# Attention's late work at other places of its steps, one table on a queue of its own, half of the first weight unit by VectorE, and the sums of k in one burst

## The chip, the cores and the metric

The kernel runs on one core of a Trainium2 chip. The metric is the device time of one execution in microseconds, from its first to its last instruction and a little around them. The core's engines are TensorE (PE, with its weight loads listed apart as PEld), VectorE (DVE), ScalarE (ACT), GpSimd (POOL) and SyncE (SP), which issues most of the transfers. Each works through its own list of instructions in order.

## What is computed

A trunk of two layers on 512 positions of width 1024, in float32. Layer 0 mixes by a Conformer convolution module, layer 1 by native sparse attention; a SwiGLU FFN of width 2816 follows each.

```python
for i in range(DEPTH):
    h = rmsnorm(x, norm_mix[i])
    y = conformer_conv_module(h, ...) if i % 4 == 0 else nsa_attention(h, ...)
    x = x + y
    x = x + swiglu_ffn(rmsnorm(x, norm_ffn[i]), ffn_w_in[i], ffn_w_out[i])
```

The attention has 16 heads of 64 in 4 groups and three branches, weighed by sigmoid gates: a compressed one (31 blocks of 32 positions, put through a small MLP), a selected one and a window. With 512 positions there are 8 blocks to select and up to 16 may be chosen, so selected and window are both plain causal attention, each with its own k and v.

```python
o_c = softmax(q @ k_cmp * scale, cmp_end <= t) @ v_cmp
o_s = softmax(q @ k_slc * scale, tok <= t) @ v_slc
o_w = softmax(q @ k_win * scale, 0 <= rel < 512) @ v_win
return g[0] * o_c + g[1] * o_s + g[2] * o_w
```

## The kernel before

The state x lies transposed, as eight tiles of 128 features by 512 positions. All weight products are made of split numbers: a factor is a high part (what the fast format of PE holds) and a low part, the rest, and one product is three matmuls (high by high, high by low, low by high). The weights come in units of up to 128x1024 through SP's queue as `wr`; ACT makes the high part `wh`, DVE the low part `wl` (`w_dma`, `w_hi`, `w_lo`, `next_w`, L244 to L281). Nearly all instructions run through one wrapper, so that their line in the profile is L153, and they are told apart by their tiles.

The start: `vec` (gains and biases) and x0 are the first two transfers of SP's queue, unit 0 is the third; ACT loads its function table in the meantime. For each of the eight x tiles ACT and DVE make `hh` and `hl`, and PE multiplies with units 0 to 3.

Layer 1's projections of q, k and v follow the FFN of layer 0. The tables `BESIDE` and `V_BESIDE` put side work beside the products of a unit: names such as `s0123` (sums of squares of k's tiles 0 to 3, tile `psq`) or `y0` and `e0` (parts of the compressed MLP), with the place in the unit.

Attention's main part is a loop over n = 1 to 17 (L2054 to L2090). There are 16 units of work, one for each pair (j, br): j is one of eight tiles of two heads, br the branch (1 selected, 2 window). Step n, three stages deep:

- scores of unit n: for each head (par 0, 1) and for t = 3, 2, 1, 0 the two matmuls of `S`, 128 query rows by 128(t+1) keys. DVE masks S into `Pm` and takes its peak `mx` in one custom instruction, ACT takes the exponential and its sum. Where br is 1, thus in even steps, t = 0 makes the columns for both branches, and the window's go to `P0` (a step with odd n has no score for t = 0). The S tiles go round three PSUM buffers.
- `weigh_late`: DVE's reciprocal of the sums, and on POOL two products that weigh Pm by it and by the gate.
- `flip` of unit n−1 (its heads are `ua`, `ub`): PE transposes blocks of Pm into `T`; `t2` and `t0` are copied out by ACT, `t1` by DVE. T shares three PSUM buffers (pool `p2`) with `psc`, `pct` and `bc`.
- `values` of unit n−2: twelve matmuls into `O`; after the second branch `out_parts` splits O into `oh` (ACT) and `ol` (DVE). `ol` and some other low parts are put off by `behind`, and issued at the next `catch_up`.

The order of each step is that of the code: S(0,3), S(0,2), S(0,1), a weigh, catch_up and values, S(0,0), flip t2, a fill, flip t1 of ua, a weigh, S(1,3), flip t1 of ub, a weigh, S(1,2), S(1,1), S(1,0), a weigh, a fill, flip t0 of ua and of ub, out_parts. Here S(p,t) is the score of head p. A fill is a piece of the list `FILL`, two to a step: the parts of the next pair of query tiles' compressed attention (`P1` to `P3`: scores `psc`, softmax by way of `cm`, `sc` and `cl`, transposes `pct`), norms `n4` to `n7` of q (`bc` among them, which DVE multiplies into `qraw`), k's later work, and at the end two weight units of the product to come (`w0`, `w1`). Within these steps every engine is held to the order of the program.

Of the kernel before, what the change touches and what calls it, by code (L numbers as in the profile page):

```python
# [19 lines left out]
P = 128  # L20
T = 512
# [71 lines left out]
    (("ga", "w", "s0", "s1 b1"), ("", "s2 s3 w", "gb s4 l", "s5 st1"), ("s6 l", "s7 l", "sc", "")))  # L93
# [4 lines left out]
FILL = ("tr0 P1.0  P1.1 P1.2  P1.3 P1.4  n4 P1.5+d3  k3+P2.0 n5  P2.1+d5 P2.2  k5 P2.4  n6 P2.5  P2.3 n7  "  # L98
        "P3.0 P3.1  P3.2 P3.3  wd P3.4  P3.5 w0  w1").split()
# [66 lines left out]
def trunk(ctx: ExitStack, tc: tile.TileContext, A, out):  # L166
# [77 lines left out]
    def w_dma(i):  # L244
        if i in raws or i >= len(units):
            return
        ap, cols, _ = units[i]
        t = wp.tile([P, 1024], F32, tag="wr", name=f"wr{i}")
        nc.sync.dma_start(t[:, :cols], ap)
        raws[i] = t  # L250
# [36 lines left out]
    nc.scalar.activation(dummy[:, :1], zb[:, :1], AF.Copy)  # L287
    vec = cst.tile([P, NVEC], F32, name="vec")
    nc.sync.dma_start(vec, A["vec"])
# [148 lines left out]
    def conv_module():  # L438
        acc = new_acc()
        with ExitStack() as cx:  # L440
# [33 lines left out]
            hold[0] = True  # L474
            for k in range(NK):
                if k < NK - 1:
                    split_x(k, V_NM0)
                if k == NK - 2:
                    split_x(NK - 1, V_NM0)
                if k % 2 == 0:  # L480
                    wh, wl = next_w(False)
                if k == 0:
                    load_tables()
                for m in range(2):
                    c = slice(k % 2 * 256 + m * P, k % 2 * 256 + (m + 1) * P)
                    mm3(pend[m], wh[:, c], wl[:, c], hh[k], hl[k], k == 0, k == NK - 1)
# [850 lines left out]
    def nsa(acc, cosT, sinT, gnext):  # L1337
# [140 lines left out]
        def square(e, ps):  # L1478
            sqs[e] = kp.tile([P, T], F32, tag="qsq", name=nm("qsq"), bufs=SQB)
            nc.scalar.activation(sqs[e], ps, AF.Square)  # L1480
# [76 lines left out]
        def split_1(q, eng):  # L1557

            hi, lo = (qk.tile([P, T], F32R, tag="q2", name=nm(z), bufs=Q2B) for z in ("qh", "ql"))
            if eng is nc.scalar:  # L1560
                eng.activation(hi, q, AF.Copy)
            else:
                eng.tensor_copy(hi, q)
            nc.gpsimd.tensor_tensor(lo, q, hi, ALU.subtract)
            return hi, lo

        def k_move(c):
            box["k2", c] = split_1(ks[c], nc.scalar)
# [82 lines left out]
        def q_pair(p):  # L1651
# [56 lines left out]
            if p == 0:  # L1708
                return move, scores, stacks, soft_a, soft_c, trans
            return [lambda: (move(0), scores(0)), lambda: (stacks(0), scores(1)), lambda: (move(1), soft_a()),  # L1710
                    lambda: stacks(1), soft_c, trans]
# [41 lines left out]
        extra["s0123"] = lambda: sums("k", range(4), 6)  # L1753
        extra["s45"] = lambda: sums("k", (4, 5), 6)
# [248 lines left out]
        fill_ = list(FILL)  # L2003
# [5 lines left out]
        def pair_(p, i):  # L2009
            if i == 0:  # L2010
                pairs[p] = q_pair(p)
            pairs[p][i]()

        for p in range(1, 4):
            for i in range(6):
                extra[f"P{p}.{i}"] = lambda p=p, i=i: pair_(p, i)
# [7 lines left out]
        def run_fill():  # L2024
            catch_up()
            if fill_:
                run(fill_.pop(0).replace("+", " "))
# [26 lines left out]
        for n in range(1, N + 2):  # L2054
# [9 lines left out]

            sc_(0, 3, 2, 1)
            weigh_late()
            if n > 1:
                catch_up()
                values(U.pop(n - 2))
            sc_(0, 0)  # L2070
            if F:
                ua, ub = U[n - 1]
                flip(((ua, 2), (ub, 2)), "t2", nc.scalar)
            run_fill()
            if F:
# [6 lines left out]
            if n == 1:  # L2082
                catch_up(1)
            sc_(1, 2, 1, 0)
            weigh_late()
            run_fill()
            if F:
                flip(((ua, 0),), "t0", nc.scalar)
                flip(((ub, 0),), "t0", nc.scalar)
            out_parts()  # L2090
# [204 lines left out]
```

## Time and profile before

| | before |
|---|---|
| runs | 1159.14, 1160.72, 1163.09 us; median 1160.72 |
| the profiled execution | 1159.72 us, span 1158.0 us |
| granted clock of TensorE | 1.000 |
| attention's seventeen steps | about 648 to 778 us of the span |
| busy: DVE, ACT, POOL | 75%, 51%, 35% of the span |
| moved through memory | 164.27 MB, mean 142 GB/s |

The page gives busy times of each engine, then the span in 40 slices, the queues, the chain of work that ended last, and groups of instructions. A row of the timeline has its start in us from the span's start, its duration, engine, line, operation, the tile written and those read with their shapes, and in brackets how long the engine stood idle before it and what it waited for. Matmuls overlap, so that the distance from one start to the next, not the duration, is what one costs in a row.

### The profile page before, as it was taken

How to read it: one execution, taken by the hardware profiler on the slowest of the kernel's cores; microseconds unless marked ns; L12 is line 12 of the kernel's file. 1: busy time of each engine (PE TensorE's matmuls, PEld its weight loads, DVE VectorE, ACT ScalarE, POOL GpSimd, SP SyncE). 2: the span in 40 equal slices, each digit the busy share in tenths (PEclk: the TensorE clock that was granted, in tenths of full speed). 3: DMA queues.
4: the chain of work that ended last, by engine and by line, in shares of the span. 5: the costliest groups of instructions: out<-in, count | busy, mean ns of one | idle time of the engine just before them, and what ended most of it. 6: DMA issues, size and time to landing. Idle time of an engine off the chain costs nothing.

```text
span 1158.0 us, 21725 instructions
## 1 busy us (share of the span) xinstructions
PE 1151.8 (99%) x8341; PEld 1010.2 (87%) x8341; DVE 863.9 (75%) x1554; ACT 586.8 (51%) x1120; POOL 404.2 (35%) x441
## 2 busy tenths in 40 slices
PE   9999999999999999999999999999999999999998
PEld 7888788899999988998779877768889999998898
DVE  7898787998777567875676778764699877756566
ACT  6322454565555444454333687773455555544443
POOL 1029122054444101233232577752304444430031
PEclk9999999999999999999999999999999999999999
DMA  9745437287777532534373232112736777762342
GB/s 365 272 126 126 97 101 208 91 208 192 192 192 197 156 114 88 162 109 114 89 171 107 56 74 56 38 38 89 202 105 164 205 192 195 192 187 93 108 128 73
DMA packets 86552, 164.27 MB, mean 142 GB/s; under 512 B 36656, under 2 KB 37808, under 8 KB 85680
## 3 DMA queue, kind: packets, MB, share of 16 engines
q1 hardware_dynamic: 66944, 108.52, 30.3%
q0 software_dynamic: 19504, 54.37, 19.8%
q8 instruction: 65, 1.06, 0.4%
q14 instruction: 39, 0.32, 0.1%
HBM read 147.23 MB, written 5.28 MB: 132 GB/s over the span
## 4 chain that ended last, share of the span: by engine, by line
PE 97%; DVE 1%; POOL 1%; issue 0%; ACT 0%; POOLq 0%; ACTq 0%
PE st L153 50%; PE pp L153 30%; PE O L153 3%; PE T L153 3%; PE S L153 3%; PE cpe L153 2%; PE pv L153 2%; POOL Pm L153 1%; PE warm L153 1%; PE psc L153 1%; DVE Pm L153 0%; PE z L153 0%; DVE t L153 0%; PE psq L153 0%; PE rbc L153 0%; PE lng L153 0%
## 5 line engine op out<-in xcount | busy, mean ns | idle before, releaser
L153 PE MATMUL st<-ball,sh 128*128 128x256 f32 x1760 | 304.8, 275 | 0.0
L153 PEld LDWEIGHTS st<-ball,sh 128*128 128x128 f32 x1760 | 264.8, 188 | 1.3 <-ACT c L153 1.0
L153 PE MATMUL st<-ball,sl 128*128 128x256 f32 x880 | 242.1, 275 | 0.0
L153 DVE TENSOR_TENSOR wl<-wr,wh 128x1024 fp32r<-128x1024 f32 (+3 forms) x144 | 178.2, 1237 | 84.5 <-ACT wh L153 84.4
L153 ACT ACTIVATE wh<-wr 128x1024 fp32r<-128x1024 f32 (+3 forms) x144 | 148.8, 1033 | 171.4 <-PE st L153 60.2
L153 POOL DMA_DIRECT2D S<-fw_x x88 | 78.3, 891 | 276.1 <-DVE sl L153 219.5
L153 POOL TENSOR_TENSOR S<-S,wr 128x512 f32<-128x512 f32 x84 | 118.7, 1413 | 147.9 <-DMA wr<-fw_op 119.3
L153 PEld LDWEIGHTS st<-ball,sl 128*128 128x128 f32 x880 | 165.2, 188 | 0.0
L153 PE MATMUL pp<-hh,wh 128*128 128x512 f32 x384 | 153.0, 398 | 0.1
L153 PE MATMUL pp<-hh,wl 128*128 128x512 f32 x384 | 149.8, 390 | 0.0
L153 PE MATMUL pp<-hl,wh 128*128 128x512 f32 x384 | 149.8, 390 | 0.0
L153 DVE TENSOR_TENSOR sl<-S,sh 128x512 fp32r<-128x512 f32 x176 | 117.9, 710 | 30.1 <-ACT sh L153 29.1
L153 PE MATMUL st<-ball,wh 128*128 128x256 f32 x704 | 124.1, 275 | 0.0
L153 ACT ACTIVATE sh<-S 128x512 fp32r<-128x512 f32 x176 | 101.0, 620 | 18.5 <-PE st L153 15.0
L153 PE MATMUL st<-row,wh 128*128 128x512 f32 x352 | 108.4, 389 | 0.0
L153 PEld LDWEIGHTS st<-ball,wh 128*128 128x128 f32 x704 | 106.2, 188 | 0.3
L153 PE MATMUL st<-ball,wl 128*128 128x256 f32 x352 | 96.8, 275 | 0.0
L153 POOL TENSOR_SCALAR Pm<-Pm,mx,gates 128x512 f32<-128x512 f32 (+2 forms) x112 | 72.9, 663 | 45.5 <-DVE mx L153 26.8
L153 PEld LDWEIGHTS pp<-hh,wh 128*128 128x128 f32 x384 | 72.2, 188 | 18.6 <-issue 2.8
L153 PEld LDWEIGHTS pp<-hh,wl 128*128 128x128 f32 x384 | 72.1, 188 | 16.2 <-DVE wl L153 0.9
L153 PEld LDWEIGHTS pp<-hl,wh 128*128 128x128 f32 x384 | 72.3, 188 | 14.6 <-issue 0.2
L153 ACT ACTIVATE c<-st 128x256 f32<-128x256 f32 x132 | 48.8, 379 | 64.8 <-PE st L153 49.5
(266 smaller groups left out, 2169.3 us busy)
## 6 DMA issues: line engine op xcount, KB each, us to landing
S<-fw_x POOLq DMA_DIRECT2D x88, 512.0 KB, 6.1
wr<-fw_in SPq DMA_DIRECT2D x44, 512.0 KB
wr<-fw_or SPq DMA_DIRECT2D x28, 512.0 KB
r<-fw_x SPq DMA_DIRECT2D x44, 256.0 KB
bd<-bands POOLq DMA_DIRECT2D x6, 1280.0 KB, 18.1
wr<-cw_in SPq DMA_DIRECT2D x14, 512.0 KB
wr<-fw_s SPq DMA_DIRECT2D x8, 512.0 KB
wr<-fw_op SPq DMA_DIRECT2D x8, 512.0 KB
```

What stands on the lines that cost most here:

```text
L153: z = f(*a, **kw)
```

## The change

It moves work in attention's steps. `FILL` becomes a table by step with three places: 0 behind the flip of t2, 1 ahead of the flips of t0, 2 behind them. The parts of a pair get names (`s0`, `s1`: the split on POOL; `m0`, `m1`: the stacking transfers; `c0`, `c1`: the compressed scores; `a`, `c`: the softmax; `t`: the transposes) and stand one by one. `catch_up` now goes with places 0 and 1 and no longer ahead of `values`. One weigh moves from behind three scores to the top of the step. The low part of k's tile 5 goes from POOL to DVE. The sums of k's squares become one burst of six tiles, beside unit 6, and `y0`, `e0` go one unit later. At the start `vec` goes to ACT's queue, ahead of ACT's function table; DVE makes the high and the low part of the left half of unit 0 by itself, ACT and DVE the right half; and the three matmuls of a product are taken in another order.

```diff
@@ -78,8 +78,8 @@
     2: {"b": "vc w"},
     3: {"b": "w r0 r1"},
     4: {"b": "w r2", 3: "m1 h1"},
-    5: {"b": "w i1 f0 r3", 3: "s0123", 5: "y0 e0"},
-    6: {"b": "w f1 r4", 4: "s45 ak", 5: "y1", 6: "e1", 7: "tk"},
+    5: {"b": "w i1 f0 r3", 6: "y0 e0"},
+    6: {"b": "w f1 r4", 4: "sK ak", 5: "y1", 6: "e1", 7: "tk"},
     7: {"b": "ck w", 5: "bk r5"},
     8: {2: "n0 n1 mv w r6", 6: "N2 N3"},
     9: {"b": "x2 x3 d2 w r7", 4: "N4 N5 x4 x5"},
@@ -90,13 +90,27 @@
 }
 V_BESIDE = (
     (("w r12", "st0", "p2m", "sABCD a1"), ("w sa", "t1", "r13 c1", ""), ("w", "", "", "")),
-    (("ga", "w", "s0", "s1 b1"), ("", "s2 s3 w", "gb s4 l", "s5 st1"), ("s6 l", "s7 l", "sc", "")))
+    (("ga", "w", "s0", "s1 b1"), ("", "s2 s3 w", "gb s4 l", "s5 st1"), ("s6 l", "s7 l", "l sc", "")))
 EVAC_V = ((1, 3), ())
 V_BANK = (2, 3, 0, 1)
 STK_P = (0,)
 
-FILL = ("tr0 P1.0  P1.1 P1.2  P1.3 P1.4  n4 P1.5+d3  k3+P2.0 n5  P2.1+d5 P2.2  k5 P2.4  n6 P2.5  P2.3 n7  "
-        "P3.0 P3.1  P3.2 P3.3  wd P3.4  P3.5 w0  w1").split()
+FILL = {
+    1: ("", "tr0 P1.c0", "cu"),
...
+    4: ("P1.c", "", "P1.t"),
+    5: ("d3", "k3 n5 P2.c0"),
...
+}
 SQB = 4
 Q2B = 4
 
@@ -241,12 +255,12 @@
     def parted(ins):
         return ins if hold[0] == "pe" else held(ins)
 
-    def w_dma(i):
+    def w_dma(i, eng=None):
         if i in raws or i >= len(units):
             return
         ap, cols, _ = units[i]
         t = wp.tile([P, 1024], F32, tag="wr", name=f"wr{i}")
-        nc.sync.dma_start(t[:, :cols], ap)
+        (eng or nc.sync).dma_start(t[:, :cols], ap)
         raws[i] = t
 
     def w_hi(i):
@@ -284,9 +298,9 @@
     zb = cst.tile([P, P], BF16, name="zb")
     nc.vector.memset(zb, 0.0)
     dummy = cst.tile([P, 8], F32, name="dummy")
-    nc.scalar.activation(dummy[:, :1], zb[:, :1], AF.Copy)
     vec = cst.tile([P, NVEC], F32, name="vec")
-    nc.sync.dma_start(vec, A["vec"])
+    tc.keep_in_program_order(nc.scalar.dma_start(vec, A["vec"]))
+    tc.keep_in_program_order(nc.scalar.activation(dummy[:, :1], zb[:, :1], AF.Copy))
     x = [xp.tile([P, T], F32, tag=f"x{m}", name=f"x{m}") for m in range(NK)]
     for m in range(NK):
         nc.sync.dma_start(x[m], A["xT"][m])
@@ -472,18 +486,45 @@
 
             pend = [pm.tile([P, T], F32, tag="pm", name=nm("pp")) for _ in range(2)]
             hold[0] = True
+
+
+            def first_w():
+                cols = units[0][1]
+                state["next"] = 1
+                hi, lo = split[0]
+                b = slice(cols // 2, cols)
+                held(nc.scalar.activation(hi[:, b], raws[0][:, b], AF.Copy))
+                held(nc.vector.tensor_tensor(lo[:, b], raws[0][:, b], hi[:, b], ALU.subtract))
+                los.add(0)
+                for k in range(4):
+                    w_dma(k)
+                return hi, lo
+
+            hi, lo = (wp.tile([P, 1024], F32R, tag=t, name=f"{t}0", bufs=2) for t in ("wh", "wl"))
+            split[0] = (hi, lo)
+            a = slice(0, units[0][1] // 2)
+            held(nc.vector.tensor_copy(hi[:, a], raws[0][:, a]))
+            held(nc.vector.tensor_tensor(lo[:, a], raws[0][:, a], hi[:, a], ALU.subtract))
             for k in range(NK):
                 if k < NK - 1:
                     split_x(k, V_NM0)
                 if k == NK - 2:
                     split_x(NK - 1, V_NM0)
-                if k % 2 == 0:
+                if k == 0:
+                    wh, wl = first_w()
+                elif k % 2 == 0:
                     wh, wl = next_w(False)
                 if k == 0:
                     load_tables()
+                    for w, z in ((wh, hh), (wl, hh), (wh, hl)):
+                        for m in range(2):
+                            held(nc.tensor.matmul(pend[m], w[:, m * P:(m + 1) * P], z[0], start=w is wh and z is hh,
+                                                  stop=False))
+                    continue
                 for m in range(2):
                     c = slice(k % 2 * 256 + m * P, k % 2 * 256 + (m + 1) * P)
-                    mm3(pend[m], wh[:, c], wl[:, c], hh[k], hl[k], k == 0, k == NK - 1)
+                    for w, z in ((wh, hh), (wl, hh), (wh, hl)):
+                        held(nc.tensor.matmul(pend[m], w[:, c], z[k], start=False, stop=z is hl and k == NK - 1))
             for k in range(NK):
                 if k == 3:
                     w_hi(state["next"])
@@ -1476,7 +1517,8 @@
                 nc.sync.dma_start(rot[b + 8:b + 16], q[b:b + 8])
 
         def square(e, ps):
-            sqs[e] = kp.tile([P, T], F32, tag="qsq", name=nm("qsq"), bufs=SQB)
+            sqs[e] = (qk.tile([P, T], F32, tag="q2", name=nm("qsq"), bufs=Q2B) if e in (4, 5) else
+                      kp.tile([P, T], F32, tag="qsq", name=nm("qsq"), bufs=SQB))
             nc.scalar.activation(sqs[e], ps, AF.Square)
 
         def first_out():
@@ -1554,18 +1596,18 @@
                 after(z, lead)
                 lead = lead or z
 
-        def split_1(q, eng):
+        def split_1(q, eng, low=nc.gpsimd):
 
             hi, lo = (qk.tile([P, T], F32R, tag="q2", name=nm(z), bufs=Q2B) for z in ("qh", "ql"))
             if eng is nc.scalar:
                 eng.activation(hi, q, AF.Copy)
             else:
                 eng.tensor_copy(hi, q)
-            nc.gpsimd.tensor_tensor(lo, q, hi, ALU.subtract)
+            low.tensor_tensor(lo, q, hi, ALU.subtract)
             return hi, lo
 
         def k_move(c):
-            box["k2", c] = split_1(ks[c], nc.scalar)
+            box["k2", c] = split_1(ks[c], nc.scalar, nc.vector if c == 5 else nc.gpsimd)
 
         def k_stack(c):
             br, a = divmod(c, 2)
@@ -1707,8 +1749,8 @@
 
             if p == 0:
                 return move, scores, stacks, soft_a, soft_c, trans
-            return [lambda: (move(0), scores(0)), lambda: (stacks(0), scores(1)), lambda: (move(1), soft_a()),
-                    lambda: stacks(1), soft_c, trans]
+            return dict(s0=lambda: move(0), s1=lambda: move(1), m0=lambda: stacks(0), m1=lambda: stacks(1),
+                        c0=lambda: scores(0), c1=lambda: scores(1), a=soft_a, c=soft_c, t=trans)
 
         extra, bcs = {}, {}
 
@@ -1750,8 +1792,7 @@
             extra[f"e{c}"] = lambda c=c: cmp_v3(c)
         extra["yc"] = cmp_k
         extra["mv"] = lambda: cmp_move(0)
-        extra["s0123"] = lambda: sums("k", range(4), 6)
-        extra["s45"] = lambda: sums("k", (4, 5), 6)
+        extra["sK"] = lambda: (sums("k", range(4), 6), sums("k", (4, 5), 6))
         extra["s6789"] = lambda: sums(0, range(6, 10), 4)
         extra["sABCD"] = lambda: sums(1, range(10, 14), 4)
         for i, (g, n, scale) in enumerate((("k", 12, 1.0), (0, 8, -SCALE), (1, 8, -SCALE))):
@@ -2000,19 +2041,18 @@
 
         us = [(j, br) for j in range(8) for br in (1, 2)]
         N = len(us)
-        fill_ = list(FILL)
         U = {}
         oh, ol = [], []
 
         pairs = {}
 
         def pair_(p, i):
-            if i == 0:
+            if p not in pairs:
                 pairs[p] = q_pair(p)
             pairs[p][i]()
 
         for p in range(1, 4):
-            for i in range(6):
+            for i in ("s0", "s1", "m0", "m1", "c0", "c1", "a", "c", "t"):
                 extra[f"P{p}.{i}"] = lambda p=p, i=i: pair_(p, i)
         extra["wd"] = lambda: [w_dma(state["next"] + i) for i in range(3)]
         for i in range(2):
@@ -2021,10 +2061,10 @@
         extra["l"] = weigh_late
         extra["-"] = lambda: None
 
-        def run_fill():
-            catch_up()
-            if fill_:
-                run(fill_.pop(0).replace("+", " "))
+        def run_fill(n, i):
+            if i < 2:
+                catch_up()
+            run((FILL.get(n, ()) + ("", "", ""))[i])
 
         def start(n):
             j, br = us[n]
@@ -2062,31 +2102,32 @@
                     for t in ts:
                         score(U[n][par], t)
 
+            weigh_late()
             sc_(0, 3, 2, 1)
-            weigh_late()
+            if F:
+                ua, ub = U[n - 1]
+            if n == N:
+                flip(((ua, 1), (ua, 3)), "t1", nc.vector)
             if n > 1:
-                catch_up()
                 values(U.pop(n - 2))
             sc_(0, 0)
             if F:
-                ua, ub = U[n - 1]
                 flip(((ua, 2), (ub, 2)), "t2", nc.scalar)
-            run_fill()
-            if F:
+            run_fill(n, 0)
+            if S:
                 flip(((ua, 1), (ua, 3)), "t1", nc.vector)
             weigh_late()
             sc_(1, 3)
             if F:
                 flip(((ub, 1), (ub, 3)), "t1", nc.vector)
             weigh_late()
-            if n == 1:
-                catch_up(1)
             sc_(1, 2, 1, 0)
             weigh_late()
-            run_fill()
+            run_fill(n, 1)
             if F:
                 flip(((ua, 0),), "t0", nc.scalar)
                 flip(((ub, 0),), "t0", nc.scalar)
+            run_fill(n, 2)
             out_parts()
         catch_up()
         order[0] = False
```

The even steps as DVE does them. Step 4, around the masks of S(0,0) and up to that of S(1,3) (`P` is P0, `ISA` the masking instruction and the accumulator read behind it; S_7657 and S_7656 are S(0,0), S_7683 and S_7685 are S(1,3)), before:

```order
L153 TENSOR_TENSOR ol_7618<-O_7416,oh_7617 128x512
L153 ISA Pm_7624,mx_7620<-S_7657,mask 128x128
L153 ISA mx_7620 128x1
L153 ISA P_7070,mx_7622<-S_7657,mask 128x128
L153 ISA mx_7622 128x1
L153 TENSOR_TENSOR qraw_6674<-qraw_6674,bc_7670 128x512
L153 COPY t_7674<-T_7673 128x512
L153 RECIPROCAL mx_7620<-mx_7620 128x2
L153 ISA Pm_7625,mx_7621<-S_7683,mask 128x512
L153 ISA mx_7621 128x1
```

And now:

```order
L167 ISA P_7072,mx_7622<-S_7656,mask 128x128
L167 ISA mx_7622 128x1
L167 TENSOR_TENSOR ol_7618<-O_7414,oh_7617 128x512
L167 TENSOR_REDUCE cl_7670<-sc_7368 128x16
L167 RECIPROCAL cl_7670<-cl_7670 128x16
L167 TENSOR_TENSOR cl_7670<-cl_7670,gates 128x16
L167 COPY t_7676<-T_7675 128x512
L167 RECIPROCAL mx_7620<-mx_7620 128x2
L167 ISA Pm_7625,mx_7621<-S_7685,mask 128x512
L167 ISA mx_7621 128x1
```

The product with bc has gone to the end of step 3. The split of O, which stood ahead of S(0,0)'s masks, and the three instructions of `cl`, which stood at the end of step 3, are between P0 and the copy of T.

PE in step 5, an odd one, from the transposes of ua's and ub's t1 to the two of t0 (T_7845 and T_7852 before, T_7843 and T_7850 now), before:

```order
L153 MATMUL T_7818<-cc,Pm_7625 128x128 x4
L153 MATMUL S_7828<-kh_6579,St_7441 128x384
L153 MATMUL S_7828<-kl_6582,St_7441 128x384
L153 MATMUL S_7833<-kh_6579,St_7441 128x256
L153 MATMUL S_7833<-kl_6582,St_7441 128x256
L153 MATMUL bc_7842<-qys_7129,er 128x512
L153 MATMUL T_7845<-cc,Pm_7624 128x128 x4
L153 MATMUL T_7852<-cc,Pm_7625 128x128 x4
```

And now:

```order
L167 MATMUL T_7797<-cc,Pm_7625 128x128 x4
L167 MATMUL S_7807<-kh_6581,St_7487 128x384
L167 MATMUL S_7807<-kl_6584,St_7487 128x384
L167 MATMUL S_7812<-kh_6581,St_7487 128x256
L167 MATMUL S_7812<-kl_6584,St_7487 128x256
L167 MATMUL bc_7833<-qys_7131,er 128x512
L167 MATMUL psc_7837<-kcb_6795,qraw_6676 128x64 x4
L167 MATMUL T_7843<-cc,Pm_7624 128x128 x4
L167 MATMUL T_7850<-cc,Pm_7625 128x128 x4
```

psc has moved from the first fill to the second, behind bc, so that two tiles other than T take buffers of p2 ahead of the transposes of t0.

More of the change, by code (lines that the diff above doesn't have):

```diff
@@ L96 @@
 STK_P = (0,)
-FILL = ("tr0 P1.0  P1.1 P1.2  P1.3 P1.4  n4 P1.5+d3  k3+P2.0 n5  P2.1+d5 P2.2  k5 P2.4  n6 P2.5  P2.3 n7  "
-        "P3.0 P3.1  P3.2 P3.3  wd P3.4  P3.5 w0  w1").split()
+FILL = {
+    1: ("", "tr0 P1.c0", "cu"),
+    2: ("P1.s0", "P1.m0 P1.c1"),
+    3: ("P1.a P1.s1", "P1.m1 n4"),
+    4: ("P1.c", "", "P1.t"),
+    5: ("d3", "k3 n5 P2.c0"),
+    6: ("P2.s0", "P2.m0 P2.c1 d5"),
+    7: ("k5 P2.a P2.s1", "P2.m1 n6"),
+    8: ("P2.c", "", "P2.t"),
+    9: ("", "n7 P3.c0"),
+    10: ("P3.s0", "P3.m0 P3.c1"),
+    11: ("P3.a P3.s1", "P3.m1"),
+    12: ("P3.c", "wd", "P3.t"),
+    13: ("", "w0"),
+    15: ("w1",),
+}
 SQB = 4
```

## The prediction

> **What bounds the kernel now.** I read the page's busy times first, then its chain, then the attention steps by windows and waits.
>
> ```profile
> span 1158.0 us, 21725 instructions
> PE 1151.8 (99%) x8341; PEld 1010.2 (87%) x8341; DVE 863.9 (75%) x1554; ACT 586.8 (51%) x1120; POOL 404.2 (35%) x441
> PE 97%; DVE 1%; POOL 1%; issue 0%; ACT 0%; POOLq 0%; ACTq 0%
> 648.00:778.00 130.00, 128.50 (x877) 94.09 (x876) 97.82 (x367) 103.58 (x308) 94.14 (x141) 1.00 0.21 50
> PE T L153 <- POOL Pm L153: 0.8, 2, 0.5
> PE T L153 <- DVE mx L153: 0.4, 1, 0.4
> PE O L153 <- ACT t L153: 0.2, 1, 0.2
> ```
>
> TensorE is busy 99% of the span and carries 97% of the chain. The fourth row is the window of attention's seventeen steps (PE, PEld, DVE, ACT, POOL busy, then the granted clock 1.00): PE stands still for 130.00 − 128.50 = 1.5 us there. The last three rows are all that the view of waits gives for PE from 640 to 780 us: total, times, longest. The change adds and removes no matmul, so all it can win in attention is such gaps. All it can lose is new ones. VectorE has 32 us of slack in the window, but slack helps only where it stands ahead of the instruction that PE needs; the even steps show that it is used up there.
>
> **The even steps, 4 and 8.** Rows of DVE, then PE's and PEld's, around the end of step 4 (start, duration):
>
> ```profile
> 674.23 0.67 DVE L153 TENSOR_TENSOR ol<-O,oh 128x512 fp32r<-128x512 f32 x1
> 675.47 0.29 DVE L153 CUSTOM_DVE_ANT_0 Pm<-S,mask 128x128 f32<-128x128 f32 x1 [0.57 <-PE S L153]
> 675.90 0.09 DVE L153 DVE_READ_ACCUMULATOR2_ANT mx<- 128x1 f32 x1
> 676.14 0.69 DVE L153 TENSOR_TENSOR qraw<-qraw,bc 128x512 f32<-128x512 f32 x1 [0.16 <-PE bc L153]
> 676.74 0.68 DVE L153 COPY t<-T 128x512 f32<-128x512 f32 x1
> 677.35 0.15 DVE L153 RECIPROCAL mx<-mx 128x2 f32<-128x2 f32 x1
> 677.42 0.67 DVE L153 CUSTOM_DVE_ANT_0 Pm<-S,mask 128x512 f32<-128x512 f32 x1
> 678.01 0.08 DVE L153 DVE_READ_ACCUMULATOR2_ANT mx<- 128x1 f32 x1
> 674.92 0.39 PE L153 MATMUL S<-kh,St 128*128 128x256 f32 x1
> 678.15 0.19 PEld L153 LDWEIGHTS S<-kh,St 128*128 128x128 f32 x1 [0.21 <-DVE mx L153]
> 671.59 0.67 DVE L153 TENSOR_REDUCE cl<-sc 128x16 f32<-128x512 f32 x1
> 672.29 0.25 DVE L153 RECIPROCAL cl<-cl 128x16 f32<-128x16 f32 x1
> 672.58 0.22 DVE L153 TENSOR_TENSOR cl<-cl,gates 128x16 f32<-128x16 f32 x1
> ```
>
> S has three PSUM buffers, so the last score of a step, S(1,0), must wait until DVE has read S(1,3): the load of its weights at 678.15 waited 0.21 us for the accumulator read that ended the 512-wide mask at 678.01. This place is already tight. Behind P0 (675.90) DVE does the bc product, the copy of T, a reciprocal and the mask. The change takes bc's product away (676.14 to 676.74, 0.60) with the 0.16 wait for it, and puts four instructions there: `ol` (an operation of the same shape as bc's product: 0.60), the sum of `cl` (672.29 − 671.59 = 0.70), its reciprocal (672.58 − 672.29 = 0.29) and its product (0.22). Until now `ol` ran at 674.23, ahead of a wait of 0.57 us for PE, and so cost nothing; this cover is gone. Counted from S(0,0) at 674.92: P0 is done at about +1.00; then 0.60 + 0.70 + 0.29 + 0.22, the copy 677.35 − 676.74 = 0.61, the reciprocal 677.42 − 677.35 = 0.07, the mask 678.01 − 677.42 = 0.59, and 678.15 − 678.01 = 0.14 to PE, together +4.22. S(1,0) stands at 678.15 − 674.92 = 3.23 now. So +0.99 us in step 4, and as much in step 8, where the order is the same: +2.0 (bounds: 0 if the `cl` chain runs before PE gets to S(1,0) in some other slack, 2.5 if its data come late).
>
> **Steps 6, 10, 12, 14.** Steps 6 and 10 get `ol` alone there, 0.60, in the place of DVE's read of psc, which is a shorter operation (128x256); I take +0.2 each, between 0 and 0.6. Step 12 gets `ol` and the three of `cl`, as step 4 does, and has no bc. Step 14 gets `ol` and the low part of a whole weight unit:
>
> ```profile
> 758.60 0.39 PE L153 MATMUL S<-kh,St 128*128 128x256 f32 x1
> 761.44 0.39 PE L153 MATMUL S<-kh,St 128*128 128x256 f32 x1
> 763.38 1.20 DVE L153 TENSOR_TENSOR wl<-wr,wh 128x1024 fp32r<-128x1024 f32 x1
> 764.50 0.68 DVE L153 CUSTOM_DVE_ANT_0 Pm<-S,mask 128x512 f32<-128x512 f32 x1
> ```
>
> Step 14's two scores are 761.44 − 758.60 = 2.84 apart. The unit costs 764.50 − 763.38 = 1.12, so S(1,0) comes at 1.00 + 1.12 + 0.60 + 0.61 + 0.07 + 0.59 + 0.14 = 4.13: +1.3. Step 12 by the same 2.84: 4.22 − 2.84 = +1.4, and I give back 0.5 for step 13, which loses the compressed transposes and DVE's work with them: +0.9. Sum of the even steps: 2.0 + 0.4 + 0.9 + 1.3 = **+4.6**.
>
> **Steps 5 and 9.** bc and psc now stand together ahead of the two transposes of t0, and with T in the same three buffers, the second of these (T of ub) takes bc's place: it waits for DVE's product with bc. Step 5 as it runs now:
>
> ```profile
> 683.87 0.65 PE L153 MATMUL T<-cc,Pm 128*128 128x128 f32 x4
> 684.36 1.00 PE L153 MATMUL psc<-kcb,qraw 128*128 128x64 f32 x8
> 685.20 0.61 PE L153 MATMUL T<-cc,Pm 128*128 128x128 f32 x4
> 687.38 1.21 PE L153 MATMUL T<-cc,Pm 128*128 128x128 f32 x8
> 689.12 0.17 DVE L153 RECIPROCAL mx<-mx 128x2 f32<-128x2 f32 x1 [0.43 <-ACT Pm L153]
> 689.21 0.67 DVE L153 TENSOR_TENSOR qraw<-qraw,bc 128x512 f32<-128x512 f32 x1
> 689.79 0.68 DVE L153 CUSTOM_DVE_ANT_0 Pm<-S,mask 128x512 f32<-128x512 f32 x1
> ```
>
> The product starts at 689.21 because the reciprocal ahead of it waits for ACT's exponential, and is done at 689.79, 5.92 behind the T at 683.87. With psc (685.20 − 684.36 = 0.84) no longer ahead, all of it comes 0.84 earlier, at 5.08, and PE goes on at 5.22. PE itself would be at the second T after half of the eight transposes, 687.38 + 0.48 − 683.87 = 3.99, with psc moved and not added. So +1.2; I take +1.1 for each of the two, +2.2 in all. Bounds: 0 if DVE's product goes ahead of the reciprocal in effect, +1.4 if all behind it slips too.
>
> **Steps 1, 3, 7.** Here the change wins. By weighing ub's t0 earlier and POOL's splits later it takes these away:
>
> ```profile
> 651.65 0.63 PE L153 MATMUL T<-cc,Pm 128*128 128x128 f32 x4 [0.40 <-DVE mx L153]
> 668.81 0.66 PE L153 MATMUL T<-cc,Pm 128*128 128x128 f32 x4 [0.28 <-POOL Pm L153]
> 703.05 0.66 PE L153 MATMUL T<-cc,Pm 128*128 128x128 f32 x4 [0.52 <-POOL Pm L153]
> ```
>
> In all 1.2 us. Step 1 gets the wait of steps 5 and 9 in a weaker form (T of ub behind DVE's read of psc, and psc behind ACT's copy of T, estimated at 0.9 together), so about 0.9 comes back: −0.3. The last steps, 15 to 17, lose little work from DVE's queue: −0.2, between −0.4 and +0.7. Attention: 4.6 + 2.2 − 0.3 − 0.2 = **+6.3**.
>
> **Start and sums.**
>
> ```profile
> 0.75 0.39 SPq L289 DMA_DIRECT2D vec<-vec  x1
> 1.19 0.42 SPq L292 DMA_DIRECT2D x<-xT  x1
> 5.39 0.80 PE L153 MATMUL pp<-hh,wh 128*128 128x512 f32 x1
> 7.90 0.63 ACT L153 ACTIVATE wh<-wr 128x512 fp32r<-128x512 f32 x1 [0.71 <-DMA wr<-cw_s]
> 556.47 1.06 PE L153 MATMUL psq<-qsq,sel 128*32 128x512 f32 x8
> 557.47 0.50 PE L153 MATMUL pp<-hh,wh 128*128 128x512 f32 x1
> ```
>
> With `vec` on ACT's queue x0 is issued at 0.75 and not at 1.19: 0.44 us at most, since unit 1 is awaited anyway (the 7.90 row) and its bytes stand behind the same transfers. DVE's half of unit 0 lets the first product (5.39) go earlier, but that only lengthens the wait for unit 1. I take −0.3, from −0.45 to +0.1. [...] The burst of k's sums at 556.47 holds PE for 557.47 − 556.47 = 1.00 us; merging it with the second one saves one change between kinds of matmul, a third of that: −0.3 (−0.5 to 0). Moving k's c=5 low part from POOL to DVE and y0, e0 by one unit I cost at nothing: each lies beside some 10 us of products per unit, and DVE is 75% busy.
>
> Sum: 6.3 − 0.3 − 0.3 = +5.7. The profiled execution took 1159.72 us (span 1158.0), 1.00 below the median of the runs, 1160.72. The difference goes on the median: 1160.72 + 5.7 = **1166.4 us**. A difference within 0.3% (3.5 us) is about what a measurement of this kernel can't tell from none.
>
> **Rivals.** *Gaps closed, nothing opened (faster).* Here S(1,0) and T of ub have more room than I count, as when the buffers of S and T are handed out in another turn. Then the 1.5 us of gaps go, with −0.3 and −0.3 besides: −2.1, for 1158.6. Some waits hide behind PE's own pipelining (the load at 678.15 waits 0.21 and no PE gap is listed); if another microsecond of these goes, −3.1 to −3.5, for 1157.4, and only there is it faster by over 0.3%. Against it stands that same 0.21: the gate binds before anything is put ahead of it. *Half (no change).* DVE's added work delays S(1,0) in steps 4 and 8 alone, and T of ub hardly: 2.0 + 0.4 − 0.5 − 0.6 = +1.3, for 1162. So it goes if DVE stands a microsecond further ahead in steps 12 and 14 than their rows show, and if the product with bc comes before PE reaches T. *More (slower still).* DVE's lateness in an even step isn't made up before the next step's scores: with 0.6 us (one `ol`) carried over in six steps, 5.7 + 3.6 = +9.3, for 1170. For it speaks that DVE had only 0.57 us idle at 675.47; against, that a stalled PE gives it time. *Not what it says.* That an order written out doesn't come into force I leave out: the order of each engine is fixed in program order in these steps.
>
> **How the numbers follow.** Forecast, with its own range 1164.2 to 1168.8 (the bounds of steps 5 and 9, the tail and the start): 0.55. More: 0.15. Half: 0.2. Gaps closed: 0.1, of which 0.08 is faster by over 0.3%, if runs scatter as they did (1159.14 to 1163.09). Slower is 0.55 + 0.15 and 0.01 of half: 0.71; same 0.21. The range 1160 to 1171 leaves out the gain, the lower edge of the middle case and the end of the worst, some 2 in 10.
>
> **What would show it.** Right: PEld S<-kh waiting for DVE mx for over 1 us in steps 4, 8, 12 and 14, T waiting for DVE qraw in steps 5 and 9, and no T<-POOL Pm in steps 3 and 7; PE's gaps in attention's window up from 1.5 to about 8 us. Wrong: PE busy 128 of 130 us there again; or a new wait named for ACT or POOL in steps that I cost at nothing.

## The result, and the profile after

The changed kernel takes 1166.36 us (median of 5 runs, 1166.00 to 1166.84), the kernel before 1160.72 (5 runs, 1159.14 to 1163.09). The ratio is 1.0052, with a 95% interval of 1.0041 to 1.0063: slower by half a per cent. The profiled execution's span went from 1158.0 to 1164.4 us.

The page's first lines and chain for the kernel after:

```profile
span 1164.4 us, 21744 instructions
PE 1149.7 (99%) x8341; PEld 1010.8 (87%) x8341; DVE 866.0 (74%) x1557; ACT 586.3 (50%) x1120; POOL 400.0 (34%) x440
PE 94%; DVE 3%; ACT 1%; issue 1%; DMA 0%; POOL 0%; SPq 0%; DVEq 0%; ACTq 0%; POOLq 0%
```

PE has as many matmuls as before, 8341. Its share of the chain fell from 97% to 94%, DVE's rose from 1% to 3%: PE waits for DVE now. Where it does so, the window of attention's steps (7 us longer than the one of before, for the steps take longer) and PE's waits from 640 to 790 us tell:

```profile
648.00:785.00 137.00, 127.61 (x876) 94.48 (x876) 98.90 (x368) 103.91 (x309) 90.27 (x140) 1.00 0.20 47
PE S L167 <- DVE mx L167: 4.8, 4, 1.2
PE T L167 <- DVE qraw L167: 2.4, 2, 1.2
PE T L167 <- POOL Pm L167: 0.6, 1, 0.6
PE T L167 <- DVE mx L167: 0.4, 1, 0.4
PE bc L167 <- DVE t L167: 0.4, 1, 0.4
PE T L167 <- DVE sc L167: 0.3, 1, 0.3
PE psc L167 <- ACT t L167: 0.2, 1, 0.2
```

PE stands still for 137.00 − 127.61 = 9.4 us where it stood 1.5. Two waits hold 7.2 of these: four times the last score S(1,0) for DVE's peak, twice T for DVE's product with bc. So the waits named as signs of a right forecast came, and T's waits for POOL in steps 3 and 7 went; the 0.6 for POOL in the list above stands in step 16, which had none. From the last matmul of v's second half to the first product behind the loop it is 137.19 us now and was 130.42: the attention is 6.8 us longer, and the whole span 6.4.

Step 4, DVE's rows from P0 to the mask of S(1,3), and PE's rows of S(0,0) and S(1,0):

```profile
675.27 0.29 DVE L167 CUSTOM_DVE_ANT_0 P<-S,mask 128x128 f32<-128x128 f32 x1
675.49 0.69 DVE L167 TENSOR_TENSOR ol<-O,oh 128x512 fp32r<-128x512 f32 x1
676.09 0.68 DVE L167 TENSOR_REDUCE cl<-sc 128x16 f32<-128x512 f32 x1
676.80 0.25 DVE L167 RECIPROCAL cl<-cl 128x16 f32<-128x16 f32 x1
677.09 0.18 DVE L167 TENSOR_TENSOR cl<-cl,gates 128x16 f32<-128x16 f32 x1
677.18 0.68 DVE L167 COPY t<-T 128x512 f32<-128x512 f32 x1
677.86 0.67 DVE L167 CUSTOM_DVE_ANT_0 Pm<-S,mask 128x512 f32<-128x512 f32 x1
678.45 0.08 DVE L167 DVE_READ_ACCUMULATOR2_ANT mx<- 128x1 f32 x1
674.51 0.39 PE L167 MATMUL S<-kh,St 128*128 128x256 f32 x1
678.59 0.39 PE L167 MATMUL S<-kh,St 128*128 128x256 f32 x1 [1.20 <-DVE mx L167]
```

The copy of T starts 677.18 − 675.49 = 1.69 us behind the end of P0, which is `ol` (0.60) and the three of `cl` (1.09) without a gap, and S(1,0) starts 678.59 − 674.51 = 4.08 us behind S(0,0), against 3.23 before. In step 5 PE's and DVE's rows are:

```profile
683.70 1.09 PE L167 MATMUL T<-cc,Pm 128*128 128x128 f32 x8
688.99 0.63 PE L167 MATMUL T<-cc,Pm 128*128 128x128 f32 x4 [1.20 <-DVE qraw L167]
688.10 0.17 DVE L167 RECIPROCAL mx<-mx 128x2 f32<-128x2 f32 x1 [0.43 <-ACT Pm L167]
688.18 0.67 DVE L167 TENSOR_TENSOR qraw<-qraw,bc 128x512 f32<-128x512 f32 x1
688.76 0.42 DVE L167 SCALAR_TENSOR_TENSOR sc<-psc,cc 128x256 f32<-128x256 f32 x1
```

The T of ub goes on when DVE's product with bc is done, and this has waited behind a reciprocal that waits for ACT: 688.99 − 683.70 = 5.29 us from the step's first T.

### The profile page after: what moved, and what is told of

Same layout as the page of the kernel before. It is cut to its first block, busy times and chain, and to the rows that moved or that the text cites. A ratio compares the mean times of both kernels' runs of the same rounds, so it can differ in the third digit from the quotient of the medians.

```text
span 1164.4 us, 21744 instructions
## 1 busy us (share of the span) xinstructions
PE 1149.7 (99%) x8341; PEld 1010.8 (87%) x8341; DVE 866.0 (74%) x1557; ACT 586.3 (50%) x1120; POOL 400.0 (34%) x440
## 4 chain that ended last, share of the span: by engine, by line
PE 94%; DVE 3%; ACT 1%; issue 1%; DMA 0%; POOL 0%; SPq 0%; DVEq 0%; ACTq 0%; POOLq 0%
PE st L167 49%; PE pp L167 30%; PE O L167 3%; PE cpe L167 2%; PE S L167 2%; PE T L167 2%; PE pv L167 2%; ACT Pm L167 1%; DVE Pm L167 1%; DVE t L167 1%; DMA x<-xT 0%; PE psc L167 0%; PE z L167 0%; POOL Pm L167 0%; PE psq L167 0%
## 5 line engine op out<-in xcount | busy, mean ns | idle before, releaser
L167 DVE TENSOR_TENSOR wl<-wr,wh 128x1024 fp32r<-128x1024 f32 (+4 forms) x145 | 178.5, 1231 | 84.1 <-ACT wh L167 84.0
L167 ACT ACTIVATE wh<-wr 128x1024 fp32r<-128x1024 f32 (+4 forms) x144 | 148.6, 1032 | 171.1 <-PE st L167 60.2
L167 POOL TENSOR_SCALAR Pm<-Pm,mx,gates 128x512 f32<-128x512 f32 (+2 forms) x112 | 69.9, 638 | 45.7 <-DVE mx L167 33.3
```

What stands on the lines that cost most here:

```text
L167: z = f(*a, **kw)
```

## The experiments

Two theories stood first. Mine: the place of DVE's instructions decides, those ahead of the mask of S(1,3) for S(1,0), and that with bc for T. The rival: DVE as a whole is late in these steps, so that the same work costs the same wherever it stands. All ratios are to the kernel before, timed alongside on the same chip (medians 1159.94 to 1160.11 us); with 1.0052 the changed kernel stands at about 1166.0 there.

### The low parts back ahead of values

```diff
             if n > 1:
+                catch_up()
                 values(U.pop(n - 2))
```

> The changed kernel with one line put back: a catch_up ahead of values, so that ol (and step 14's low part of a weight unit) again runs on DVE while it waits for S(0,0). Theory (what DVE has between P0 and the 512-wide mask of S(1,3) sets when S(1,0) may start): the waits of S(1,0) fall from 1.36 to about 0.76 us in steps 4, 8 and 12, from 0.27 to 0 in 6 and 10, from 1.39 to 0 in 14, together -3.7 us: about 1162.6. Rival (DVE as a whole is late in these steps, and the same work on it in another place slips just as much): the waits move and the time stays within 1 us of 1166.4.

Measured: 1162.71 us, ratio 1.0023 (1.0014 to 1.0032). The view of PE's waits has, of S, in this kernel:

```profile
PE S L167 <- DVE mx L167: 1.8, 3, 0.6
```

S(1,0) comes 3.48 us behind S(0,0) in steps 4, 8 and 12 (4.08 with the change alone), and 2.83 in 6, 10 and 14 (2.98, 2.98 and 4.11). That is 0.60, the length of `ol`, in the first three, and all of the wait in the others. The rival, that nothing changes, is out: DVE does the same work.

### The softmax's second half one place earlier

```diff
-    3: ("P1.a P1.s1", "P1.m1 n4"),
-    4: ("P1.c", "", "P1.t"),
+    3: ("P1.a P1.s1", "P1.m1 n4", "P1.c"),
+    4: ("", "", "P1.t"),
```

The same for P2 from step 8 to 7 and for P3 from 12 to 11.

> The changed kernel with the second half of the softmax (P1.c, P2.c, P3.c: three DVE instructions of cl and one POOL product) put one place earlier, at the end of steps 3, 7 and 11. Theory: the three cost 677.18 - 676.09 = 1.09 us ahead of the copy of T in step 4; S(1,0)'s waits in steps 4, 8 and 12 fall by that from 1.36 to 0.27, -3.3 us, with 0 to 0.3 given back in each next step, where the first masks come later: 1163.1 to 1164. Rival (DVE as a whole is late): within 1 us of 1166.4.

Measured: 1162.50 us, ratio 1.0024 (1.0015 to 1.0033). S(1,0) comes 2.98, 2.98 and 3.04 us behind S(0,0) in steps 4, 8 and 12: 1.04 to 1.10 less, about the 1.09 of the three instructions, and the attention is 3.2 us shorter, so that nothing is given back.

### The compressed scores away from bc

```diff
-    5: ("d3", "k3 n5 P2.c0"),
+    5: ("d3 P2.c0", "k3 n5"),
-    9: ("", "n7 P3.c0"),
+    9: ("P3.c0", "n7"),
```

> The changed kernel with the compressed scores psc of steps 5 and 9 back at the first place of the step, so that bc stands alone ahead of the two T of t0. Theory (two foreign tiles in p2's three buffers make the T of ub wait for DVE's product with bc): the two waits of 1.36 us for DVE qraw go, -2.7 us, with up to 0.3 back for each psc: 1163.7 to 1164.3. Rival (the wait is for the weighs of ub on POOL or the exponential, and only shows as qraw): the T of ub waits as long for another releaser and the time stays at 1166.

Measured: 1164.11 us, ratio 1.0033 (1.0022 to 1.0045). No wait for qraw is left, and the stretch from the end of step 5's values to the end of step 6's, 1.21 us longer with the change than before, is as it was (8.70 us before, 8.69 here).

### The three together

> The three edits of the other runs of this call together. Theory: the waits of S(1,0) in steps 4, 8, 12 (3 x 1.36), 6 and 10 (2 x 0.27) and 14 (1.39) and of T in steps 5 and 9 (2 x 1.36) all go: -8.7 us, about 1157.7, below the kernel before, since the start's 0.46 us and the ends of the waits in steps 3 and 4 stay. Rival (DVE or POOL as a whole is late): new waits take their place and the time stays above 1160.7.

Measured: 1158.95 us, ratio 0.9990 (0.9981 to 0.9999): below the kernel before, 1.3 us above what I expected. PE's waits in this kernel:

```profile
PE T L167 <- POOL Pm L167: 0.6, 1, 0.6
PE T L167 <- DVE mx L167: 0.4, 1, 0.4
PE bc L167 <- DVE t L167: 0.4, 1, 0.4
PE T L167 <- DVE sc L167: 0.3, 1, 0.3
PE psc L167 <- ACT t L167: 0.2, 1, 0.2
PE S L167 <- DVE mx L167: 0.2, 1, 0.2
```

The two large waits are gone, and no new one has come in their place; the five others of the changed kernel stand as they were. Its attention is 129.95 us, 7.2 below the changed kernel's, and not 8.7. The 1.5 that are missing can be accounted for. The expectation counted as wait all that S(1,0) or T came later than 0.12 us behind the matmul ahead, 1.48 − 0.12 = 1.36. But where nothing waits (S(1,0) in the kernel of the section "The same work two places further on", T here) the distance is 0.24 us, so that 0.12 in each of eight places, 1.0 in all, was no wait. The other 0.5 is still there: S(1,0) starts 0.38, 0.38 and 0.45 us behind the matmul ahead in steps 4, 8 and 12.

### One part alone on the kernel before

The line that the first experiment put in, here taken out of the kernel before:

```diff
             if n > 1:
-                catch_up()
                 values(U.pop(n - 2))
```

> The kernel before with one line left out: the catch_up ahead of values, so that ol and step 14's low part of a weight unit run behind the masks of S(0,0). Nothing else of the change. Theory (DVE's work between P0 and the mask of S(1,3) sets S(1,0)): steps 4 and 8 lose 0.44 us each (0.60 less the 0.16 for which DVE waits for bc there), 6 and 10 about 0.5 each, 12 0.2 and 14 1.3, together +3.3: about 1163.2. Rival (the place of ol doesn't matter alone, only with the change's other moves): within 1 us of the kernel before, 1160.

Measured: 1162.56 us, ratio 1.0020 (1.0011 to 1.0030). PE's wait for DVE's peak, none in the kernel before, is

```profile
PE S L153 <- DVE mx L153: 2.0, 3, 1.2
```

Steps 4 and 8 lose 0.35 us each, 12 loses 0.14 and 14 loses 1.27, each within 0.1 of what was expected; steps 6 and 10 lose nothing, where I expected 0.5. There DVE reads psc behind P0, which PE makes later, and `ol` fills that wait. So the line alone costs over 2 us of the 6.8.

A second run moves psc alone in the kernel before: in steps 5 and 9 it goes behind bc, ahead of the transposes of t0.

```diff
-FILL = ("tr0 P1.0  P1.1 P1.2  P1.3 P1.4  n4 P1.5+d3  k3+P2.0 n5  P2.1+d5 P2.2  k5 P2.4  n6 P2.5  P2.3 n7  "
-        "P3.0 P3.1  P3.2 P3.3  wd P3.4  P3.5 w0  w1").split()
+FILL = ("tr0 P1.0  P1.1 P1.2  P1.3 P1.4  n4 P1.5+d3  k3 n5+P2.0  P2.1+d5 P2.2  k5 P2.4  n6 P2.5  P2.3 n7+P3.0  "
+        "- P3.1  P3.2 P3.3  wd P3.4  P3.5 w0  w1").split()
```

> The kernel before with one part of the change: in steps 5 and 9 psc is moved behind bc, ahead of the two T of t0. Theory (T of ub takes bc's buffer and waits for DVE's product with bc): two new waits of T for DVE qraw of 1.2 us, +2.4: about 1162.5. Rival (the wait needs the earlier weigh or the changed copies as well): no wait for qraw, within 0.5 us of the kernel before.

Measured: 1162.14 us, ratio 1.0019 (1.0010 to 1.0028), and this kernel's waits have

```profile
PE T L153 <- DVE qraw L153: 2.4, 2, 1.2
```

The pair of bc and psc ahead of T makes its two waits without any other part of the change.

### The same work two places further on

Here the late low parts and `cl` stay in the changed kernel's step, but stand behind the copy of T of ub, and so behind the mask of S(1,3). In `FILL`, `P1.c`, `P2.c` and `P3.c` go to a fourth place of steps 4, 8 and 12; the rest of the edit, with lines left out at the dots:

```diff
-            if i < 2:
+            if 0 < i < 2:
                 catch_up()
...
             if F:
                 flip(((ub, 1), (ub, 3)), "t1", nc.vector)
+            catch_up()
+            run_fill(n, 3) if len(FILL.get(n, ())) > 3 else None
```

> The changed kernel with its late low parts and cl's instructions moved two places on, behind the copy of T of ub; all of them stay in the same step, and nothing is taken away. Theory (only what stands ahead of the mask of S(1,3) delays S(1,0); what stands behind it delays the mask of S(1,2), whose buffer the next step's first score takes): all waits of S(1,0) go, -6.0, and the first scores of steps 5, 9, 13 and 15 wait about 0.8 us each, +3.3: -2.7, about 1163.3. Rival (DVE is late in the step as a whole, wherever the work stands): the new waits are as long as the old ones, 1166.

Measured: 1181.62 us, ratio 1.0181 (1.0167 to 1.0195): 15 us slower than the changed kernel, where I expected 2.7 faster. S(1,0) waits no more in any step, as the theory has it, but I had left out a chain: `pct` in the same step's last place needs POOL's product of sc, and this needs `cl`. This kernel's rows of PE around the first of these waits:

```profile
681.81 1.12 PE L167 MATMUL pct<-cc,sc 128*128 128x128 f32 x4 [2.05 <-POOL sc L167]
682.58 0.78 PE L167 MATMUL S<-kh,St 128*128 128x512 f32 x1
683.15 0.63 PE L167 MATMUL S<-kl,St 128*128 128x512 f32 x1
```

pct waits 2.05, 2.04 and 2.04 us in steps 4, 8 and 12; step 15's first score waits 1.82 for DVE's masks, behind the weight unit and `ol`, and a T 1.95 for POOL in step 16. And the matmuls behind this wait are slow: a score of 128x512 takes 0.78 and 0.63 us instead of 0.48 and 0.39. The last section has that. The experiment doesn't tell the two theories apart, since it brought in new waits of its own; the first two do.

### The weigh at the top of the step

In the kernel with the three edits:

```diff
-            weigh_late()
             sc_(0, 3, 2, 1)
+            weigh_late()
```

> The kernel with the three edits put back, and the weigh at the top of each step moved behind its three scores, where it stood before. Theory of the prediction (the earlier weigh took away the waits of T for POOL's Pm in steps 3 and 7, 0.28 and 0.52 us): they come back, +0.8: about 1159.7. Rival (the move of POOL's splits of q, qh and ql, took them away): within 0.2 us of the gaps of the kernel without this edit, 1158.95.

Measured: 1159.54 us, ratio 0.9994 (0.9985 to 1.0003). The waits for POOL in steps 3 and 7 did not come back. Step 1 got longer by 0.8 us, and step 7 shorter: from its first matmul of O with t to step 8's it is 8.09 us, against 8.96 with the weigh at the top and 8.18 in the kernel before. So the rival is right: the move of POOL's splits took those waits away, and the weigh at the top costs 0.9 in step 7. That gives a mixed form, against the kernel with the three edits:

```diff
-            weigh_late()
+            if n == 1:
+                weigh_late()
             sc_(0, 3, 2, 1)
+            if n > 1:
+                weigh_late()
```

> The kernel with the three edits put back, and the weigh at the top of the step in step 1 alone; from step 2 on it stands behind the three scores again. Theory (the weigh at the top helps step 1 by 0.8 us and costs step 7 0.9, as the two earlier runs differ): -0.9 in step 7, +0.2 in step 8, nothing in step 1: about 0.6 below the kernel with the three edits, 1158.3 against 1160.0 for the kernel before. Rival (the differences between those two runs were of their single profiles): within 0.2 us of 1159.

Measured: 1158.42 us, ratio 0.9985 (0.9976 to 0.9994), faster than both kernels; its attention is 129.45 us. Why does the weigh cost in step 7? In the changed kernel DVE's subtraction of `cm`, ahead of the copy of T, and POOL's split run side by side there:

```profile
702.86 1.58 DVE L167 TENSOR_TENSOR sc<-sc,cm 128x512 f32<-128x512 f32 x1
704.36 0.68 DVE L167 COPY t<-T 128x512 f32<-128x512 f32 x1
702.60 1.29 POOL L167 TENSOR_TENSOR ql<-qraw,qh 128x512 fp32r<-128x512 f32 x1
705.09 0.50 PE L167 MATMUL bc<-qys,er 128*128 128x512 f32 x1 [0.40 <-DVE t L167]
706.45 0.63 PE L167 MATMUL T<-cc,Pm 128*128 128x128 f32 x4 [0.43 <-DVE mx L167]
```

The subtraction starts when POOL has 1.03 us to go and takes 1.58 us; bc waits for the copy behind it. The earlier weigh brings POOL's split forward into DVE's subtraction. The next edit, again of the kernel with the three edits, moves the split alone.

```diff
-    7: ("k5 P2.a P2.s1", "P2.m1 n6", "P2.c"),
+    7: ("k5 P2.a", "P2.s1 P2.m1 n6", "P2.c"),
```

> The kernel with the three edits put back and the weigh at the top of every step, with POOL's split of q in step 7 (qh and ql) moved from the first place to the second; DVE's order is the same to the instruction. Theory (step 7's gaps come from a collision: DVE's subtraction of cm took 1.58 us there while POOL's ql ran, and 0.69 to 0.74 in the kernel with the weigh at the top in step 1 alone): the subtraction takes 0.7 again, the gap ahead of bc (0.57) goes and the one ahead of T shrinks, -0.85, of which up to 0.5 may come back in step 8, where the split now stands ahead of POOL's product of sc: 1158.1 to 1158.6. Rival (the weigh at the top itself makes DVE late in step 7, whatever POOL does): subtraction and gaps as in the kernel with the three edits, 1158.95.

Measured: 1158.47 us, ratio 0.9990 (0.9981 to 0.9999). DVE's order is the same; its subtraction of `cm` in step 7 of this kernel is

```profile
699.50 0.69 DVE L167 TENSOR_TENSOR sc<-sc,cm 128x512 f32<-128x512 f32 x1
```

and bc waits no more: step 7 is 0.88 us shorter than with the three edits, and nothing comes back in step 8. The attention takes 129.07 us, the shortest of all. The time itself can't be told from that of the mixed form.

### Two places of step 1 and step 7 as before

Again an edit of the kernel with the three edits:

```diff
-    1: ("", "tr0 P1.c0", "cu"),
+    1: ("tr0", "P1.c0", "cu"),
-    6: ("P2.s0", "P2.m0 P2.c1 d5"),
-    7: ("k5 P2.a P2.s1", "P2.m1 n6", "P2.c"),
+    6: ("P2.s0 P2.m0 P2.c1", "P2.a d5"),
+    7: ("k5 P2.s1", "P2.m1 n6", "P2.c"),
```

> The kernel with the three edits of the first call put back, and two places more as in the kernel before: in step 1 the compressed transposes pct in the first fill, in step 6 the scores psc in the first fill and the first half of the softmax in the second (out of step 7, where it stands ahead of the copy of T). Theory (each foreign DVE instruction ahead of a copy that PE's T or bc waits for costs its length): the gaps of 0.35 and 0.47 in step 1 and of 0.57 and 0.58 in step 7 go, less 0.2 to 0.3 that pct waits: -1.7 us against 1158.95, about 1157.3. Rival (step 7's gaps come from the low part of k's tile 5, which the change gave to DVE): only step 1's go, -0.6: 1158.4.

Measured: 1160.91 us, ratio 1.0009 (1.0000 to 1.0018): 2 us above the kernel with the three edits, and a miss. Step 1's waits in this kernel:

```profile
PE T L167 <- DVE pcl L167: 1.1, 1, 1.1
PE pct L167 <- POOL sc L167: 1.0, 1, 1.0
```

With the weigh of ub put ahead of the softmax by the change ("l sc"), POOL gets to sc 0.96 us later, counted from its first weigh, than in the kernel before (4.73 and 3.77 us), and pct in the first fill waits for it; so the change's move of pct in step 1 belongs to its move of the weigh. Step 7 got 0.7 us shorter, as expected (of its two gaps, one of 0.32 is left), but step 6 lost 0.6 of it. The rival, that k's tile 5 on DVE makes step 7's gaps, was settled by the run before: there this work still stands on DVE, and step 7 is no longer than in the kernel before.

### The start and the burst alone

The kernel before with the parts of the change outside attention's loop, but for the weigh put ahead of the softmax ("l sc").

> The kernel before with the change's parts outside attention's steps alone: vec on ACT's queue, half of unit 0 by DVE, the order of the first products, one burst of k's sums with its tiles. Theory: the start gains 0.3 to 0.5 us by the first 20 us of the trace, the burst 0.3 between its first matmul and the next product, together -0.7: about 1159.2. Rival (the first weight units arrive when they did, and PE waits for them instead): the start gains nothing behind unit 1, and the time stays at 1160.

Measured: 1159.26 us, ratio 0.9993 (0.9984 to 1.0002), against 1160.11: the sign is as expected, but the interval holds no change. In its trace the 60th product starts 0.25 us earlier than in the kernel before. In the ten other traces of kernels with that start the spread is from 0.1 later to 0.75 earlier, with 0.46 in the changed kernel's own.

## Why the prediction was right

The forecast was 1166.4 us, slower with 0.71, and 1166.36 was measured. So close an agreement is partly luck: the attention lost 6.8 us where 6.3 were forecast, single terms err in both directions, and the median of the kernel before to which the sum was added, 1160.72, lies 0.6 us or more above those of its later runs.

**The even steps**, +4.6 predicted. From S(0,0) to S(1,0), steps 4 and 8 took 0.85 us more each (0.99 predicted), step 12 took 1.25 more (1.4), step 14 1.27 more (1.3), and 6 and 10 0.14 more each without psc (0.2). That is 4.5. The 0.5 that I gave back for step 13 was wrong: the transposes pct that leave it (−0.44) come to step 12 (+0.38), and 0.06 is left. Without it the forecast for these steps would have been 5.1, so 4.6 against 4.5 is two errors that cancel. The order of DVE, priced with the durations of before, gave each step to 0.15 us. What it had too high was `cl`: 1.09 us in place of 1.21. That this chain sets the end is shown by the first two experiments and by the kernel before without its catch_up.

**A gain not foreseen in step 5.** The sixteen matmuls of O with t take 2.99 us in step 5 of the kernel before and 2.37 in the changed one. They need ACT's two copies of t0. These rows are of ACT in the kernel before:

```profile
680.67 0.19 ACT L153 ACTIVATION_READ_ACCUMULATOR Pm<-Pm,mx 128x1 f32 x1
680.76 0.58 ACT L153 ACTIVATE pch<-pct 128x512 fp32r<-128x512 f32 x1
681.24 0.62 ACT L153 ACTIVATE qh<-kraw 128x512 fp32r<-128x512 f32 x1
681.76 1.06 ACT L153 ACTIVATE t<-T 128x512 f32<-128x512 f32 x2
```

And in the changed one:

```profile
681.11 0.19 ACT L167 ACTIVATION_READ_ACCUMULATOR Pm<-Pm,mx 128x1 f32 x1
681.20 1.06 ACT L167 ACTIVATE t<-T 128x512 f32<-128x512 f32 x2
682.16 0.58 ACT L167 ACTIVATE pch<-pct 128x512 fp32r<-128x512 f32 x1
```

Before, the copies stood behind the high part of pct and behind `qh`, the high part of k's tile 3 (`d3`); now pct's stands behind them, and `d3` has gone to the next step. In step 9 of the kernel before pct's high part alone stands ahead of the copies, and O takes 2.47 us there, only 0.10 more than with the change. So most of the 0.62 seems to come from the move of `d3`, which the prediction doesn't name; no run moved one of the two alone, so this is argued, not shown.

**Steps 5 and 9**, +2.2 predicted: +1.2 each. T of ub comes 5.29 us behind the step's first T where 5.22 was predicted. The kernel before with this part alone shows it.

**Steps 1, 3, 7**, −0.3 predicted: +0.06, −0.11 and +0.78 us, together +0.7. Here a step of the prediction failed, twice. It compared S(0,0) to S(1,0) in steps 4 and 8 with and without bc's matmuls, and left out that these come back in steps 3 and 7, at about 0.3 us each: some 0.6 too little. And its reason for the gain, "by weighing ub's t0 earlier and POOL's splits later", holds for the splits alone: the weigh takes no wait away in steps 3 and 7, and in step 7 it costs 0.9 us, by the collision of POOL's split with DVE's subtraction (1.58 us in place of 0.69). The places of the split and of the softmax's first half were costed at nothing. So was the low part of k's tile 5, as lying beside products; its row on DVE stands in step 7 (699.84, 0.89 us), and that it cost nothing there, as the run with the split moved shows, was luck.

**The last steps**, −0.2 predicted: −0.1. **Start**, −0.3 predicted: −0.46 in the one trace, not settled to better than a few tenths. That 0.3 of the 0.44 us between the two issues would be won was my estimate, and no run shows it as such; ACT's first `hh` starts at 3.82 us where it started at 4.00, and now waits for `vec`. **Burst**, −0.3 predicted: two bursts held 557.47 − 556.15 = 1.32 and 565.41 − 564.11 = 1.30 us from the product ahead to the next one, one burst holds 2.23; with one usual distance of 0.23 less, −0.16. The third of 1.00 us for one change between kinds of matmul was my estimate too; no run shows such a change by itself. Between the 20th microsecond and v's last matmul traces of kernels alike in that stretch differ by up to 2 us, so that these last two terms are below what one execution shows.

**The rivals.** "Gaps closed" was half true and outweighed: the waits of step 1 for DVE's peak and of steps 3 and 7 for POOL did go, though steps 1 and 7 got others of 0.19 to 0.43 us. "More" (lateness carried into the next step) did not happen: the distance from S(1,0) to the next step's first score is 1.57 us in step 4 before and after.

## What to carry to other kernels

On an engine that works its list in order, ask of each moved instruction what stands behind it that the bounding engine waits for: the same `ol` is free while DVE waits for PE, and costs its 0.60 us behind the last instruction that gave DVE that pause. Follow a moved result to all its readers, too: two of the moves tried here made new waits of 1 to 2 us in a chain that had not been followed (from sc on POOL to pct). And a table of places is best mended part by part: three small moves back, with the rest of the change kept, gave 0.9990 and with a fourth 0.9985 of the kernel before.

## What the runs showed of the hardware

**Behind five pauses of 1.8 to 2.05 us the clock was halved.** In the kernel with the work two places further on, granted clock (the column behind the five engines) by windows around the end of the first pause of 2.05 us:

```profile
681.80:682.80 1.00, 0.99 (x5) 0.99 (x6) 0.29 (x3) 1.00 (x7) 1.00 (x3) 0.50 0.00 0
682.80:683.80 1.00, 1.00 (x4) 0.81 (x4) 0.17 (x1) 1.00 (x3) 1.00 (x2) 0.50 0.00 0
683.80:684.80 1.00, 1.00 (x6) 0.78 (x5) 0.87 (x3) 0.56 (x2) 1.00 (x3) 0.50 0.00 0
685.20:686.20 1.00, 1.00 (x12) 0.64 (x10) 0.25 (x2) 1.00 (x5) 0.00 (x0) 1.00 0.00 0
```

For 3.4 us PE ran at half clock, and was back at 1.00 then. The same came behind each of the five long pauses of that kernel's profiled execution (2.05, 2.04, 2.04, 1.82 and 1.95 us), and behind none of its two of 1.19 and 1.20, nor of the six of 1.20 to 1.22 in the changed kernel, whose attention ran at 1.00. So each of these five was paid twice. Five stretches of 3.4 us at half clock cost some 8.5 us (an estimate, half of their 17.0); PE's waits in attention are 14.2 us against 9.1 in the changed kernel, and the attention is 14.7 us longer. Neither kernel has a pause between 1.22 and 1.82 us there, and no run here shows what brings the half clock on.

**Of a subtraction of DVE and one of POOL side by side, the one begun second took longer.** DVE's subtraction of two operands in step 7 took 1.58 us beside POOL's subtraction in the changed kernel, and 0.69 without it in the run with the split moved. From 702.86 it ended at 704.44, POOL at 703.89, that is 0.55 us earlier. In steps 3 and 11 of the changed kernel it is the other way round: there DVE's subtraction starts first (666.17 and 738.15) and takes 0.69 us, and POOL's split, begun 0.20 us later, takes 1.62 us in place of 1.28. Why it is so, no run here shows.
